# A new on-chip layout for the operands of a two-block transformer kernel

## The chip, the cores and the metric

The kernel runs on one core of a Trainium2 chip. TensorE (PE in the profile) multiplies, and its weight loads have a row of their own (PEld); VectorE (DVE), ScalarE (ACT) and GpSimd (POOL) do the element work; SyncE (SP) issues the transfers from the chip's memory. The metric is the device time of one execution in microseconds, lower being better.

## What is computed

The reference sends a sequence of 256 tokens with 1024 features through two transformer blocks, in float32. Cut to what matters:

```python
# first block
h = rmsnorm(x, norm_pre_mix);  z = h @ w_in           # gating, forgetting heads, memory heads
y = concat([gmlp(z), forgetting_attention(z), memory_cross_attention(z, mem)]) @ w_out
x = x + rmsnorm(y, norm_post_mix)
f = square(relu(rmsnorm(x, norm_pre_ffn) @ w_ff1)) @ w_ff2        # 1024 -> 4096 -> 1024
x = x + rmsnorm(f, norm_post_ffn)
# second block, two layers (sliding window attention, then latent attention)
for i in range(2):
    x = x + 0.5 * swiglu(rmsnorm(x), wg1[i], wu1[i], wd1[i])      # 1024 -> 2816 -> 1024
    x = x + attention_i(rmsnorm(x))
    x = x + 0.5 * swiglu(rmsnorm(x), wg2[i], wu2[i], wd2[i])
```

## The kernel before, in words

Activations are held transposed: 128 features in the partitions, the 256 tokens along them, so x is eight tiles of 128x256 float32 (1024 bytes a partition). Every large product is made of three matmuls, since each operand is split into a high and a low half of type float32r: high times high, high weight times low activation, low weight times high activation. These are lines 137 to 139 in `mm_t` (weight block of 128x128 stationary, 256 tokens moving) and lines 147 to 149 in `mm_n` (activation block stationary, 256 to 512 weight columns moving). Of 9048 matmuls in `mm_t`, 5520 with 128 columns of weights have the normed residual `xh`/`xl` moving, 2880 the hidden layer of a feed-forward stage `ah`/`al`, and 576 the joined heads `oh`/`ol`.

The weights are streamed. `Stream` takes transfers of up to 2048 columns into three buffers (`raw`), cuts them into parts of up to 1024 columns, and splits each part: ScalarE makes the high half `wh` (line 100), VectorE the low half `wl` (line 110). There are six buffers of each, and parts are asked for four ahead. A part is 24 matmuls in the gate and up stages. The order of the work on each engine is the order in which the code is written.

On-chip memory is a stack of pools. A pool starts where the one before it ends, each tile's size is rounded up to 32 bytes a partition, and the first pool starts at byte 16512 of a partition. The pools of a stage are opened behind the standing ones, and behind them all come at byte 138240, which is 270 times 512. In the kernel before, the pool of constants (`cst`) comes first, and in it `cols` has 404 bytes and `rows` 408. What stands behind them starts as follows (byte in a partition modulo 512, as the built programs have it):

| tiles | role in the products | before | after |
|---|---|---|---|
| `raw`, `wh`, `wl` | weights | 352 | 0 |
| `x`, `xh`, `xl` | residual and its halves | 352 | 0 |
| tiles of `tp` (`t`, `f`, `sq`, `acc`, `rb`) | work tiles | 352 | 0 |
| `ah`, `al`, `oh`, `ol`, `mh`, `ml`, `ch`, `cl` | activations of a stage | 0 | 0 |
| `kon` (identity, ones) | fp32 matmuls | 32 | 0 |
| `p`, `pt` of both attention layers of the second block (in the first block they are at 0 in both) | fp32 matmuls | 160 | 256 |
| `kT`, `qT` of the latent heads | fp32 matmuls | 160 | 256 |

So before, a matmul with `xh` or `xl` moving has both of its operands at 352, and one with `ah`, `al`, `oh` or `ol` moving has the moving operand at 0 and the weights at 352. In `mm_n` the weights move, at 352, and what is loaded is `xh` at 352 or `mh` and `ch` at 0.

Of the kernel before, what the change touches and what calls it, by code (L numbers as in the profile page):

```python
# [9 lines left out]
F32 = mybir.dt.float32  # L10
F32R = mybir.dt.float32r
BF16 = mybir.dt.bfloat16
I32 = mybir.dt.int32
# [4 lines left out]
P = 128  # L18
T = 256
# [4 lines left out]
CHUNK_COLS = 2048  # L24
# [11 lines left out]
N_COLS = 101  # L36
# [14 lines left out]
def block_kernel(ctx: ExitStack, tc: tile.TileContext, a: dict, out: bass.AP, upto: int = 99):  # L51
    nc = tc.nc
    pool = lambda name, bufs, **kw: ctx.enter_context(tc.tile_pool(name=name, bufs=bufs, **kw))
    cst = pool("cst", 1)
    wp = pool("wp", 1)
    res = pool("res", 1)
    tp = pool("tp", 2)
    sm = pool("sm", 1)
    psp = pool("psp", 8, space=bass.MemoryType.PSUM)
# [3 lines left out]
    def bank():  # L63
        return psp.tile([P, 512], F32, tag="ps", name="ps")

    # weight stream -------------------------------------------------------
    order = []
    RAW, HL, AHEAD = 3, 6, 4

    class Stream:  # L70
        """Weights come in transfers of up to CHUNK_COLS columns, each cut into parts; a part is
        split into float32r halves whose sum is the float32 weight."""

# [50 lines left out]
        def fill(self):  # L124
            """As many parts as there is room for, the low part of the last still to come."""
            while self.ns < self.ng + HL and self.split(gp):
                pass

    ws = Stream()

    # products ------------------------------------------------------------
    def mm_t(ps, w, off, n, x, kts, first, last, m=P):
        h, lo = w
        for j, k in enumerate(kts):
            c = off + k * n
            s0, s1 = first and j == 0, last and j == len(kts) - 1
            pe.matmul(ps, lhsT=h[:, c:c + m], rhs=x[0][k], start=s0, stop=False)  # L137
            pe.matmul(ps, lhsT=h[:, c:c + m], rhs=x[1][k], start=False, stop=False)  # L138
            pe.matmul(ps, lhsT=lo[:, c:c + m], rhs=x[0][k], start=False, stop=s1)  # L139
# [10 lines left out]

    # constants -----------------------------------------------------------
    ctx.enter_context(tc.manual_schedule())
# [3 lines left out]
    X = (xh, xl)  # L156
    cols = cst.tile([P, N_COLS], F32, name="cols")
    kon = cst.tile([P, 3 * P], F32, name="kon")
    kmask = cst.tile([P, 768], F32, name="kmask")
    rows = cst.tile([P, N_ROWS], F32, name="rows")  # L160
    posr = cst.tile([P, T], I32, name="posr")
    posc = cst.tile([P, 64], I32, name="posc")
    posn = cst.tile([P, 2], I32, name="posn")
    relb = cst.tile([P, 2, 16], F32, name="relb")
    mhalf = cst.tile([P, 32], F32, name="mhalf")
    gp.memset(mhalf, -0.5)
# [5 lines left out]
    def gcol(i, k):  # L172
        return cols[:, i * KT + k:i * KT + k + 1]
# [3 lines left out]

    # norms ---------------------------------------------------------------
    def rstd_pow(dst, src, n):
        gp.tensor_tensor(out=dst, in0=src, in1=mhalf[:, :n], op=ALU.pow)  # L180
# [4 lines left out]
    def add_sq(acc, k, src):  # L185
        if k == 0:
            act.activation(out=acc, in_=src, func=AF.Square)
        else:
            sq = tp.tile([P, T], F32, tag="sq", name="sq")
            act.activation(out=sq, in_=src, func=AF.Square)  # L190
            gp.tensor_tensor(out=acc, in0=acc, in1=sq, op=ALU.add)  # L191
# [50 lines left out]
    def prep(k, g, acc):  # L242
        """High part of a tile of the next normed input now, low part of the tile before."""
        act.activation(out=xh[k], in_=x[k], func=AF.Copy, scale=gcol(g, k))  # L244
        if acc is not None:
            add_sq(acc, k, x[k])
        prep_end()
        late.append((k, gcol(g, k)))

    def prep_end():  # L250
        while late:
            k, g = late.pop()
            dve.scalar_tensor_tensor(out=xl[k], in0=x[k], scalar=g, in1=xh[k].bitcast(F32), op0=ALU.mult, op1=ALU.subtract)

    # attention -----------------------------------------------------------
    def attn_exp(u):
# [68 lines left out]
    class Pipe:  # L325
        """Heads in flight: each step transposes the probabilities of the head two back, scores a
        new one, multiplies the values of the head three back, and goes on with the softmaxes."""

# [44 lines left out]

    # FFN of the second block ----------------------------------------------
    def ffn2(acc, gnext, extra=(), start=None, more=()):
# [52 lines left out]
    def out_proj_start(pipe, oh, ol, sets):  # L428
        """The first four tiles of an output projection, between the last steps of the heads."""
        ps, w, todo = [bank() for _ in range(4)], [], []  # L430
        seen = 0
        for ks in sets:
            for d in range(4):
                if not seen:
                    w.append(ws.get(max(0, HL - 2 - d)))
                mm_t(ps[d][:, :T], w[d], 0, P, (oh, ol), ks, not seen, False)
                pipe.done() or pipe.step()
            seen = 1
        while not pipe.done():
            pipe.step()  # L440
        return ps, w
# [28 lines left out]
    def y_evac(d, p, y, yacc, gi):  # L470
        """One tile of a post-normed sublayer: times its gain, and its squares."""
        if d == KT - 1:
            sq = tp.tile([P, T], F32, tag="sq", name="sq")
            act.activation(out=sq, in_=p, func=AF.Square)
        else:
            sq = None
            add_sq(yacc, d, p)
        act.activation(out=y[d], in_=p, func=AF.Copy, scale=gcol(gi, d))
        return sq

    # relative position bias: a threshold mask of the distances times the steps between buckets,
    # 8 groups of 4 keys a set, sets 0-3 for the first query tile
    rbd = cst.tile([P, 3, 64], BF16, name="rbd")

# [51 lines left out]

    # ======================================================================
    seq = [("w1f", 0, 4), ("w1q", 0, 6), ("w1k", 0, 2), ("w1m", 0, 1), ("w1v", 0, 2), ("w1u", 0, 3),
# [6 lines left out]
    for nm, i0, i1 in seq:  # L545
        for i in range(i0, i1):
            src = [a[nm][i, 0], a[nm][i, 1]] if len(a[nm].shape) == 4 else [a[nm][i]]
            for ap in src:
                n = ap.shape[-1]
                cut = cuts.get(nm) or ([DN_CUT * P, n] if nm.startswith("dn") else list(range(PART, n + 1, PART)))  # L550
                order.append((ap, cut))

# [1 line left out]
    warm_table(AF.Exp)  # L554
# [20 lines left out]
    with ExitStack() as es:  # L575
        mp = es.enter_context(tc.tile_pool(name="mix", bufs=1))
# [22 lines left out]

        # values and gates of the forgetting heads (natural)  # L600
        acc = new_acc()
# [16 lines left out]

        # queries and keys of the forgetting heads
        pq = [bank() for _ in range(3)]  # L620
# [98 lines left out]

        # queries of the memory heads, memory keys and values, with the forgetting heads in between  # L720
        for i in range(2):
# [22 lines left out]
        for tt in range(2):  # L744
            act.activation(out=vm[tt], in_=pv[tt][:, :T], func=AF.Copy, scale=rs_m[:, tt:tt + 1])
        # gating branch, with the memory heads in between
        pg = [bank(), bank()]
# [51 lines left out]

        # output projection, post norm  # L800
        yacc = new_acc("macc")
# [18 lines left out]

# [1 line left out]
    with ExitStack() as es:  # L822
# [69 lines left out]

# [1 line left out]
    with ExitStack() as es:  # L894
# [34 lines left out]
        mp = es.enter_context(tc.tile_pool(name="swa", bufs=1))  # L929
# [7 lines left out]
        rq = mp.tile([P, KT, 2, 2], F32, name="rq")  # L937
        ga = mp.tile([P, 1], F32, name="ga")
        dve.scalar_tensor_tensor(out=ga, in0=cols[:, C_AQ:C_AQ + 1], scalar=0.125, in1=cols[:, C_AK:C_AK + 1],
# [91 lines left out]

# [1 line left out]
    tq = cst.tile([P, 2, 2, 32], F32, name="tq")  # L1033
    tk = cst.tile([P, 2, 2, 32], F32, name="tk")

# [32 lines left out]
    with ExitStack() as es:  # L1068
        mp = es.enter_context(tc.tile_pool(name="mla", bufs=1))
# [10 lines left out]
        ol = [mp.tile([P, T], F32R, name=f"ol{k}") for k in range(KT)]  # L1080
        gb = mp.tile([P, 1], F32, name="gb")
        rqb = mp.tile([P, 4, 2, 4], F32, name="rqb")
# [3 lines left out]
        warm_table(AF.Exp)  # L1086
        # latent projections, transposed: keys and values first
        w, w2 = ws.get(), ws.get()
# [230 lines left out]

# [1 line left out]
def _kp(w):  # L1321
# [136 lines left out]
```

## Time and profile before

| what | value |
|---|---|
| time, median of 3 runs (lowest, highest) | 1299.66 us (1294.41, 1300.59) |
| span of the profiled execution, first to last instruction | 1296.4 us |
| TensorE's mean granted clock in it | 0.989 |
| PE busy | 1270.1 us (98%) |
| PEld busy | 1223.0 us (94%) |
| DVE busy | 846.0 us (65%) |
| ACT busy | 661.6 us (51%) |
| POOL busy | 197.4 us (15%) |
| DMA queue of the weights | 47.8% of 16 engines' span, 209.78 MB |

The profiled execution's own time is known as its span; the median of the runs lies 3.3 us above it, which is start and end outside the first and last instruction and the spread between runs. A busy PE does not tell how fast it is: matmuls are pipelined, one takes some 280 ns from its start to its modelled end and the next starts long before that. What tells is the step from one start to the next, read from the timeline, or the number of matmuls in a window.

### The profile page before, as it was taken

To read this page: it belongs to the slowest core of one execution; us is meant where nothing else is said; L and a number is where in the kernel's file an instruction comes from. 1 tells how busy PE (TensorE), PEld (TensorE's weight loads), DVE (VectorE), ACT (ScalarE), POOL (GpSimd) and SP (SyncE) were. 2 spreads that over 40 slices of the span, in tenths; PEclk is the share of its full clock that TensorE was granted. 3 is DMA by queue.
4 is the path that set the end of the run, shared out by engine and by line. 5 is a ranking of instruction groups with operands and counts; after the bars stand their busy time and mean duration, and the time that the engine had idled before them with its cause. 6 is when DMAs were issued, how large, how long until landed. Compare 5 with 4: busy or idle time off the path is not lost.

```text
span 1296.4 us, 24835 instructions
## 1 busy us (share of the span) xinstructions
PE 1270.1 (98%) x10316; PEld 1223.0 (94%) x10316; DVE 846.0 (65%) x1490; ACT 661.6 (51%) x1174; POOL 197.4 (15%) x192
## 2 busy tenths in 40 slices
PE   8999899999899999999999999999999999999998
PEld 7789899999799999977999999999999878999998
DVE  6886676654686666686766556666566786666553
ACT  5556455434344544565544444545444787444442
POOL 4424210110420001210300001100001451100000
PEclk9999899999899999999999999999999989999999
DMA  7534355565145545621555556545456412555453
GB/s 230 197 117 145 115 174 193 195 222 177 57 138 200 184 149 190 218 94 34 177 201 176 174 163 210 192 172 196 165 164 199 160 65 70 188 171 191 154 196 106
DMA packets 37265, 211.37 MB, mean 163 GB/s; under 512 B 4768, under 2 KB 8224, under 8 KB 18848
## 3 DMA queue, kind: packets, MB, share of 16 engines
q1 hardware_dynamic: 37152, 209.78, 47.8%
q8 instruction: 81, 1.33, 0.4%
q14 instruction: 32, 0.26, 0.1%
HBM read 208.71 MB, written 1.05 MB: 162 GB/s over the span
## 4 chain that ended last, share of the span: by engine, by line
PE 88%; DVE 7%; issue 2%; DMA 1%; ACT 1%; POOL 0%; SPq 0%; ACTq 0%; DVEq 0%; POOLq 0%
PE ps L137 26%; PE ps L138 26%; PE ps L139 26%; DVE wl L110 3%; PE ps L289 2%; PE ps L315 2%; PE ps L300 1%; PE ps L147 1%; PE ps L148 1%; PE ps L149 1%; DMA raw<-in_w1k 1%; PE ps L317 1%; DMA raw<-in_w1f 0%; DVE dg L226 0%; ACT wh L100 0%
## 5 line engine op out<-in xcount | busy, mean ns | idle before, releaser
L137 PE MATMUL ps<-xh,wh 128*128 128x256 f32 (+1 forms) x1848 | 529.6, 287 | 1.6 <-ACT xh L525 1.6
L138 PE MATMUL ps<-xl,wh 128*128 128x256 f32 (+1 forms) x1848 | 527.1, 285 | 1.4 <-DVE xl L532 0.9
L139 PE MATMUL ps<-xh,wl 128*128 128x256 f32 (+1 forms) x1848 | 525.7, 284 | 2.0 <-DVE wl L110 2.0
L110 DVE TENSOR_TENSOR wl<-raw,wh 128x1024 fp32r<-128x1024 f32 (+3 forms) x434 | 489.3, 1166 | 48.1 <-ACT wh L100 46.5
L100 ACT CAST wh<-raw 128x1024 fp32r<-128x1024 f32 (+4 forms) x436 | 400.2, 957 | 67.0 <-PE ps L138 28.6
L137 PEld LDWEIGHTS ps<-xh,wh 128*128 128x128 f32 (+1 forms) x1848 | 356.6, 193 | 5.3 <-issue 3.2
L138 PEld LDWEIGHTS ps<-xl,wh 128*128 128x128 f32 (+1 forms) x1848 | 356.5, 193 | 3.4 <-DVE xl L532 2.3
L139 PEld LDWEIGHTS ps<-xh,wl 128*128 128x128 f32 (+1 forms) x1848 | 356.8, 193 | 2.2 <-DVE wl L110 2.2
L137 PE MATMUL ps<-ah,wh 128*128 128x256 f32 x960 | 268.6, 280 | 0.0
L138 PE MATMUL ps<-al,wh 128*128 128x256 f32 x960 | 268.6, 280 | 0.0
L139 PE MATMUL ps<-ah,wl 128*128 128x256 f32 x960 | 268.5, 280 | 0.0
L137 PEld LDWEIGHTS ps<-ah,wh 128*128 128x128 f32 x960 | 180.5, 188 | 0.0
L138 PEld LDWEIGHTS ps<-al,wh 128*128 128x128 f32 x960 | 180.5, 188 | 0.0
L139 PEld LDWEIGHTS ps<-ah,wl 128*128 128x128 f32 x960 | 180.5, 188 | 0.0
L385 ACT ACTIVATE s<-t 128x256 f32<-128x256 f32 x88 | 36.8, 418 | 204.3 <-DVE t L383 204.3
L191 POOL TENSOR_TENSOR acc<-acc,sq 128x256 f32<-128x256 f32 x42 | 49.9, 1188 | 598.2 <-ACT sq L190 598.1
L383 DVE TENSOR_TENSOR t<-ps,rb 128x256 f32<-128x256 f32 x88 | 37.2, 423 | 85.4 <-PE ps L139 79.9
L205 DVE TENSOR_TENSOR al<-f,ah 128x256 fp32r<-128x256 f32 (+1 forms) x105 | 48.9, 466 | 52.8 <-ACT ah L204 52.8
L204 ACT CAST ah<-f 128x256 fp32r<-128x256 f32 (+1 forms) x105 | 45.9, 437 | 55.7 <-DVE f L387 43.1
L244 ACT ACTIVATE xh<-x,cols 128x256 fp32r<-128x256 f32 x40 | 20.4, 510 | 101.8 <-DVE x L420 94.7
L387 DVE TENSOR_TENSOR f<-ps,s 128x256 f32<-128x256 f32 x88 | 37.3, 424 | 47.4 <-ACT s L385 47.4
L419 DVE SCALAR_TENSOR_TENSOR t<-ps,rb 128x256 f32<-128x256 f32 x32 | 13.6, 424 | 77.1 <-PE ps L139 77.1
(285 smaller groups left out, 1322.8 us busy)
## 6 DMA issues: line engine op xcount, KB each, us to landing
raw<-in_gu SPq DMA_DIRECT2D x88, 1024.0 KB, 5.0
raw<-in_dn SPq DMA_DIRECT2D x64, 704.0 KB, 4.3
raw<-in_ff SPq DMA_DIRECT2D x32, 1024.0 KB, 4.9
raw<-in_w_out SPq DMA_DIRECT2D x4, 1024.0 KB, 4.9
raw<-in_aq SPq DMA_DIRECT2D x4, 1024.0 KB, 5.0
raw<-in_a_out SPq DMA_DIRECT2D x4, 1024.0 KB, 4.8
raw<-in_b_out SPq DMA_DIRECT2D x4, 1024.0 KB, 4.9
raw<-in_w1q SPq DMA_DIRECT2D x6, 512.0 KB, 3.9
```

What stands on the lines that cost most here:

```text
L100: act.copy(h[:, :n], t)
L110: eng.tensor_tensor(out=lo, in0=t, in1=h.bitcast(F32), op=ALU.subtract)
L137: pe.matmul(ps, lhsT=h[:, c:c + m], rhs=x[0][k], start=s0, stop=False)
L138: pe.matmul(ps, lhsT=h[:, c:c + m], rhs=x[1][k], start=False, stop=False)
L139: pe.matmul(ps, lhsT=lo[:, c:c + m], rhs=x[0][k], start=False, stop=s1)
L191: gp.tensor_tensor(out=acc, in0=acc, in1=sq, op=ALU.add)
L204: act.copy(h, src)
L205: dve.tensor_tensor(out=lo, in0=src, in1=h.bitcast(F32), op=ALU.subtract)
L289: pe.matmul(ps[:, o:o + n], lhsT=u["q"][:, i * P:i * P + P], rhs=u["k"][:, :n], start=True, stop=True)
L383: dve.tensor_tensor(out=t, in0=g, in1=rb, op=ALU.mult)
L385: act.activation(out=s, in_=t, func=AF.Silu)
L387: dve.tensor_tensor(out=f, in0=u, in1=s, op=ALU.mult)
```

## The change

No instruction is added, removed or moved on any engine, and every wait is for the same engine as before; only addresses differ. The small tiles whose sizes add up to 896 bytes come first in a pool of their own (`lead`), then the weight stream, the residual and the work tiles; the other constants follow those, the two of odd size (`cols`, `rows`) and `posn` last. `tq` and `tk` are allocated with them and not later. `ga` and `gb` are the first column of a tile of 32 columns. Comments and docstrings that go are left out here.

```diff
-    cst = pool("cst", 1)
+    lead = pool("lead", 1)
     wp = pool("wp", 1)
     res = pool("res", 1)
     tp = pool("tp", 2)
+    cst = pool("cst", 1)
     sm = pool("sm", 1)
...
-    cols = cst.tile([P, N_COLS], F32, name="cols")
+
+    mhalf = lead.tile([P, 32], F32, name="mhalf")
+    rbd = lead.tile([P, 3, 64], BF16, name="rbd")
+    relb = lead.tile([P, 2, 16], F32, name="relb")
+    posc = lead.tile([P, 64], I32, name="posc")
     kon = cst.tile([P, 3 * P], F32, name="kon")
     kmask = cst.tile([P, 768], F32, name="kmask")
+    posr = cst.tile([P, T], I32, name="posr")
+    tq = cst.tile([P, 2, 2, 32], F32, name="tq")
+    tk = cst.tile([P, 2, 2, 32], F32, name="tk")
+    cols = cst.tile([P, N_COLS], F32, name="cols")
     rows = cst.tile([P, N_ROWS], F32, name="rows")
-    posr = cst.tile([P, T], I32, name="posr")
-    posc = cst.tile([P, 64], I32, name="posc")
     posn = cst.tile([P, 2], I32, name="posn")
-    relb = cst.tile([P, 2, 16], F32, name="relb")
-    mhalf = cst.tile([P, 32], F32, name="mhalf")
...
-    rbd = cst.tile([P, 3, 64], BF16, name="rbd")
...
-        ga = mp.tile([P, 1], F32, name="ga")
+        ga = mp.tile([P, 32], F32, name="ga")[:, 0:1]
...
-    tq = cst.tile([P, 2, 2, 32], F32, name="tq")
-    tk = cst.tile([P, 2, 2, 32], F32, name="tk")
...
-        gb = mp.tile([P, 1], F32, name="gb")
+        gb = mp.tile([P, 32], F32, name="gb")[:, 0:1]
```

## Rows read from the trace of the kernel before

**Rows 1.** The page: span, busy time by engine, granted clock by slice

```profile
span 1296.4 us, 24835 instructions
...
PE 1270.1 (98%) x10316; PEld 1223.0 (94%) x10316; DVE 846.0 (65%) x1490; ACT 661.6 (51%) x1174; POOL 197.4 (15%) x192
...
PEclk9999899999899999999999999999999989999999
```

**Rows 2.** The chain of waits, shares of the span by line

```profile
by line: PE ps L137 26.0%; PE ps L138 25.7%; PE ps L139 25.5%; DVE wl L110 2.7%; PE ps L289 2.1%; issue 2.0%; PE ps L315 1.8%; PE ps L300 1.3%; PE ps L147 0.9%; PE ps L148 0.8%; PE ps L149 0.8%; DMA raw<-in_w1k 0.6%; PE ps L317 0.6%; DMA ra
```

**Rows 3.** Groups of PE instructions by shape: busy us, mean ns, idle before

```profile
L137 PE MATMUL ps<-xh,wh 128*128 128x256 f32 x1840 | 527.3, 287 | 1.6 <-ACT xh L525 1.6
...
L137 PE MATMUL ps<-ah,wh 128*128 128x256 f32 x960 | 268.6, 280 | 0.0
...
L137 PE MATMUL ps<-oh,wh 128*128 128x256 f32 x192 | 55.4, 288 | 0.0
```

**Rows 4.** Windows: length, then busy us and count (x) by engine, clock, DMA

```profile
160.00:220.00 60.00, 60.00 (x502) 60.00 (x502) 41.51 (x46) 34.52 (x50) 6.81 (x8) 1.00 0.55 186
255.00:315.00 60.00, 60.00 (x514) 60.00 (x513) 27.66 (x25) 24.67 (x33) 8.15 (x10) 1.00 0.55 195
655.00:735.00 80.00, 80.00 (x669) 80.00 (x669) 48.96 (x71) 37.92 (x56) 0.00 (x0) 1.00 0.54 185
955.00:1005.00 50.00, 50.00 (x429) 50.00 (x428) 32.59 (x45) 23.39 (x38) 7.44 (x6) 1.00 0.60 194
```

**Rows 5.** Timeline of PE, 1005 to 1010 us: starts; 32 columns of weights

```profile
1008.55 0.28 PE L139 MATMUL ps<-xh,wl 128*32 128x256 f32 x1
...
1009.91 0.28 PE L139 MATMUL ps<-xh,wl 128*32 128x256 f32 x1
```

**Rows 6.** Timeline of PE, 66 to 67.5 us: weights move, mh is loaded

```profile
65.79 0.29 PE L149 MATMUL ps<-wl,mh 128*128 128x256 f32 x1
...
67.47 0.28 PE L148 MATMUL ps<-wh,ml 128*128 128x256 f32 x1
```

**Rows 7.** Timeline of PE, 77 to 77.9 us: 384 columns move, xh is loaded

```profile
76.82 0.33 PE L148 MATMUL ps<-wh,xl 128*128 128x384 f32 x1
...
77.86 0.33 PE L148 MATMUL ps<-wh,xl 128*128 128x384 f32 x1
```

**Rows 8.** Timeline of PE, 1022.5 to 1024.8 us: 384 columns, ch loaded

```profile
1022.59 0.34 PE L147 MATMUL ps<-wh,ch 128*128 128x384 f32 x1
...
1024.53 0.34 PE L149 MATMUL ps<-wl,ch 128*128 128x384 f32 x1
```

**Rows 9.** The same at half clock: timeline, and its window

```profile
1042.65 0.52 PE L148 MATMUL ps<-wh,cl 128*128 128x384 f32 x1
...
1044.89 0.52 PE L149 MATMUL ps<-wl,ch 128*128 128x384 f32 x1
...
1042.20:1045.20 3.00, 3.00 (x11) 0.50 0.00 0
```

**Rows 10.** Groups of DVE and PE by shape: other operands by address

```profile
L205 DVE TENSOR_TENSOR al<-f,ah 128x256 fp32r<-128x256 f32 x90 | 38.2, 425 | 42.5 <-ACT ah L204 42.5
...
L387 DVE TENSOR_TENSOR f<-ps,s 128x256 f32<-128x256 f32 x88 | 37.3, 424 | 47.4 <-ACT s L385 47.4
...
L420 DVE TENSOR_TENSOR x<-x,t 128x256 f32<-128x256 f32 x32 | 13.6, 426 | 1.1
...
L315 PE MATMUL ps<-pt,av 128*64 128x256 f32 x32 | 10.3, 405 | 0.0
...
L315 PE MATMUL ps<-pt,fv 128*64 128x256 f32 x12 | 3.9, 405 | 0.0
```

**Rows 11.** The chain in order of time, 340 to 400 us, its longest pieces

```profile
363.26 3.97 DVE wl L110 x2
370.69 3.97 DVE wl L110 x2
378.13 3.97 DVE wl L110 x2
```

## The prediction

> **What bounds the kernel now.** I read the page first: PE is busy 98% of a span of 1296.4 us, at full clock in nearly every slice [rows 1]. That alone says little, so the chain of waits comes next: lines 137 to 139, the three matmuls of the split products, hold 26.0 + 25.7 + 25.5 = 77.2% of the span, 1001 us, and no line of another engine, nor any transfer, holds more than 2.7% [rows 2]. The kernel is as fast as those matmuls follow each other. Their listed durations (280 to 288 ns) are not that pace, but the groups already differ by what moves, and `xh` stands at 352 where `ah` and `oh` stand at 0 [rows 3]. The pace comes from counts. A window counts whatever touches it, so its length plus one duration (0.28 us), divided by the count, is the step from start to start [rows 4]:
> - `xh`/`xl` moving at 352, weights at 352: 60.28 / 502 and 80.28 / 669, both 120.0 ns;
> - `ah`/`al` moving at 0, weights at 352: 60.28 / 514 and 50.28 / 429, both 117.3 ns.
>
> Clock, shape, type, weights and bytes are the same in the two; what differs is where the moving tile starts. So the layout does reach the pace, and 2.7 ns of it is visible before any change.
>
> **What an aligned step would be.** At half clock 384 columns step by 2.24 us over 7 steps, 320.0 ns, one column per cycle with nothing on top [rows 9]. At full clock one column per cycle would be 106.7 ns for 256 columns and 160 ns for 384, and no step of these products comes down to it: something that half the pace hides costs 10 to 16 ns. The sizes tell more. With weights of only 32 columns and both operands at 352 the step is 1.36 us over 12, 113.3 ns [rows 5]; with 128 columns 120.0 ns [rows 4]; 384 columns moving with both at 352 take 1.04 us over 6, 173.3 ns [rows 7]. Above one column per cycle these are 6.7, 13.3 and 13.3 ns: one or two times 16 columns, that is 64 bytes. 352 is 5.5 times 64. My reading is that the moving operand is fetched in pieces of 64 bytes: 1024 bytes that start in the middle of a piece touch 17, not 16, and 128 columns of weights cost one piece-time more. 16 + 1 + 1 = 18 pieces give 120.0, 17 without the second give 113.3, and 1536 bytes (25 pieces, plus 1) give 173.3. That fits all three rows where both operands stand at the same offset.
>
> Where the two stand at different offsets the step isn't a whole number of pieces: 117.3 ns is 17.6, and 384 columns moving at 352 over `ch` at 0 take 1.94 us over 11, 176.4 ns, which is more than 173.3 although one of the operands is better aligned [rows 8]. With 256 columns of weights moving at 352 over `mh` at 0 it is 1.68 us over 14, again 120.0 [rows 6]. So aligning the loaded operand alone gains nothing; the moving one alone gains 2.7 ns; both together, which is what the change makes, stand in no row. Bounds for both at 0: below, 106.7 ns (one column per cycle); above, 120.0 (what a common offset gives now). I take 113.3, which is 16 pieces plus the one for the weights: a common offset gave whole pieces in all three rows, and the half piece at the front goes.
>
> **The change part by part.**
> - `mm_t` over `xh`/`xl`, 5520 matmuls: 120.0 to 113.3, 6.7 ns each.
> - `mm_t` over `ah`, `al`, `oh`, `ol`, 3456 matmuls: 117.3 to 113.3, 4.0 ns each.
> - How many of them set the end: at the mean step of (5520 x 120.0 + 3456 x 117.3) / 8976 = 119.0 ns the chain's 1001 us are 8410 matmuls, 94% of all. So 0.94 x (5520 x 6.7 + 3456 x 4.0) = 0.94 x (37.0 + 13.8) = 48 us.
> - `mm_n` is under 3% of the chain (0.9 + 0.8 + 0.8) [rows 2], much of it waits at the start. At 4 to 6% of 2.5% of the span it gives 1 us or 2; I count 0, which leaves this on the safe side.
> - fp32 matmuls (scores, transposes, values): nothing. `pt` at 160 and `pt` at 0 both read 405 ns over 256 columns [rows 10]; they have the pace at which nothing shows.
> - VectorE and ScalarE: nothing. Operands at 352 and 0 mixed, PSUM and 0, or all at 352 read 425, 424 and 426 ns [rows 10].
> - Transfers into `raw`: no row separates their address, but the chain holds under 1% of such waits by line (0.6% for the largest) [rows 2], so even a tenth of those is near 1 us; I take 0.
> - Earlier `tq`, `tk` and wider `ga`, `gb`: no instruction and no wait differs, 0.
>
> What is late next: the split of the weights. While the buffers refill after the first block's feed-forward stage, pairs of `wl` instructions set the pace [rows 11]; such stretches are outside the 94%, yet a faster PE lengthens them. In steady stretches VectorE is busy 41.5 of 60 and 49.0 of 80 us [rows 4]; 6% less time lifts the higher from 69% to 73%, so it keeps up. I take 2 us off for the refills: 46 us. The sum is against the span of 1296.4, which becomes 1250.4; the median of the runs lies 3.3 us above that span, so the forecast is 1254 us. Its own range, for 112.5 to 114.5 ns and a path share of 85 to 97%, is 1243 to 1268.
>
> **The rivals.**
> 1. Only the moving operand counts: all products go as `ah` does now. For it: a rate of 117.3 on 2880 matmuls without exception, and `mh`, where aligning the loaded tile changed nothing. Against it: the broken 17.6 pieces, which only unequal offsets show. 0.94 x 5520 x 2.7 = 14 us, 1286.
> 2. No piece is lost at all, 106.7 to 111 ns. For it: the 32-column rows lose none to their weights. Against: they are a quarter of the load. At 109 ns: 0.94 x (5520 x 11.0 + 3456 x 8.3) = 84 us, 1216; at the bound of 106.7 1196. The Trainium skill ("TensorE: Matmul & The Clock Gate", Part 2) states two independent read ports, so that loading the next weights takes nothing from the running matmul, and a step of N/2.4 + 2.5 ns, 109.2 here; by it the sum would be this rival's. The rows disagree: narrower weights alone took 6.7 ns off.
> 3. Slower: two operands at a common offset collide, wherever that is. For it: `xh` over `wh`, both at 352, is the slowest pace and the steadiest. Then the `xh` products stay at 120.0, and those over `ah` and `oh`, which lose their unequal offset, go from 117.3 to 120.0: 0.94 x 3456 x 2.7 = 9 us more, 1309. Against it: `mh` at 0 under weights at 352 has unequal offsets and is at 120.0 too. It decides if the step in the hidden-layer stages rises above 117.3.
> 4. Nothing happens: 1300. An offset of 352 would have to be as good as 0. The comparison of `xh` and `ah` speaks against it, unless their 2.7 ns come from something else that differs between the stages, such as eight tiles used over and over. The Trainium skill ("SBUF — State Buffer", Specifications) gives lines of 16 bytes; 352 is 22 of them, so by this rule no operand moves onto a better boundary. The windows show otherwise as far as they go, 120.0 against 117.3.
>
> **How the numbers follow.** Forecast (113.3 ns) 0.45; a step between it and rival 1, around 115.5 ns and 1271 us, 0.07; rival 1 0.20; rival 2 0.13; rival 3 0.10; rival 4 0.05. A measurement of this kernel can tell about 0.5%, 6.5 us, from no change. Faster: 0.45 + 0.07 + 0.20 + 0.13 = 0.85; same is rival 4, 0.05; slower is rival 3, 0.10. The range runs from 1208, which takes in most of rival 2, to 1290, which takes in rival 1; outside stay rivals 3 and 4 and the rest of 2, under 0.2.
>
> **What would show it.** In the profile after, a window in a gate and up stage and one in a hidden-layer stage should have the same step, 113.3 ns, and it should be as even as the 120.0 is now: 532 matmuls in 60 us where there were 502 and 514. The chain should still be lines 137 to 139. The attention stages and the start should hardly move. I am wrong in the step if the two windows differ or if both read 117.3 or 120.0; wrong in the path if the step is 113.3 and the time falls by much less than 46 us, in which case the idle time before the `xh` products, now 1.6 us at line 137 [rows 3], has grown under `wl` or `raw`.

## The result, and the profile after

The changed kernel takes 1304.77 us (median of 5 runs, 1303.69 to 1305.42), the kernel before in the same series 1297.97 us (5 runs, 1294.41 to 1300.59). The ratio is 1.0057 with a 95% interval of 1.0039 to 1.0074: slower by 0.6%, where 1254 us had been forecast. That is the way of the third rival, which was priced at 1309 us and given a chance of 0.10.

The page of the changed kernel, span and busy time by engine:

```profile
span 1301.9 us, 24835 instructions
...
PE 1276.5 (98%) x10316; PEld 1230.6 (95%) x10316; DVE 846.3 (65%) x1490; ACT 661.7 (51%) x1174; POOL 196.1 (15%) x192
```

Against [rows 1] the span is 5.5 us longer, PE is busy 6.4 us longer and its weight loads 7.6 us; VectorE, ScalarE and GpSimd agree to about 1 us. The chain of waits by line (the product's lines are now 138 to 140):

```profile
by line: PE ps L138 26.3%; PE ps L139 26.0%; PE ps L140 25.9%; PE ps L294 2.2%; DVE wl L111 2.1%; issue 2.0%; PE ps L320 1.8%; PE ps L305 1.3%; PE ps L148 0.9%; PE ps L149 0.8%; PE ps L150 0.8%; DMA raw<-in_w1q 0.7%; PE ps L322 0.6%; DMA x<
```

Still the products, 78.2% where [rows 2] had 77.2%. Two groups of them by shape, and the four windows of [rows 4] (length, then busy us and count by engine, clock, DMA):

```profile
L138 PE MATMUL ps<-xh,wh 128*128 128x256 f32 x1840 | 526.6, 286 | 1.0 <-ACT xh L528 1.0
...
L138 PE MATMUL ps<-ah,wh 128*128 128x256 f32 x960 | 271.7, 283 | 0.0
```

```profile
160.00:220.00 60.00, 60.00 (x503) 60.00 (x502) 41.81 (x46) 34.53 (x50) 6.79 (x8) 1.00 0.54 188
255.00:315.00 60.00, 60.00 (x503) 60.00 (x502) 27.67 (x25) 23.65 (x30) 7.69 (x9) 1.00 0.53 187
655.00:735.00 80.00, 80.00 (x669) 80.00 (x668) 49.25 (x70) 37.46 (x56) 0.00 (x0) 1.00 0.55 188
955.00:1005.00 50.00, 50.00 (x419) 50.00 (x418) 31.55 (x46) 23.04 (x39) 6.35 (x6) 1.00 0.56 187
```

With `xh` moving nothing has changed: 669 in 80 us, 120.0 ns. With `ah` moving, 419 in 50 us where there were 429: 50.28 / 419 = 120.0 ns in place of 117.3, and a duration of 283 ns in place of 280 [rows 3]. Both kinds of product are now equally slow, which is the sign of a wrong step that the prediction named. The third rival's price for that, 0.94 x 3456 x 2.7 ns, is 9 us; 5.5 us show in the spans and 6.8 us between the medians.

### The profile page after: what moved, and what is told of

Read it like the earlier page. It is cut to its first block, busy times and chain, and to the rows that moved or that the text cites. A ratio compares the mean times of both kernels' runs of the same rounds, so it can differ in the third digit from the quotient of the medians.

```text
span 1301.9 us, 24835 instructions
## 1 busy us (share of the span) xinstructions
PE 1276.5 (98%) x10316; PEld 1230.6 (95%) x10316; DVE 846.3 (65%) x1490; ACT 661.7 (51%) x1174; POOL 196.1 (15%) x192
## 4 chain that ended last, share of the span: by engine, by line
PE 89%; DVE 6%; issue 2%; ACT 1%; DMA 1%; POOL 0%; SPq 0%; ACTq 0%; POOLq 0%; DVEq 0%
PE ps L138 26%; PE ps L139 26%; PE ps L140 26%; PE ps L294 2%; DVE wl L111 2%; PE ps L320 2%; PE ps L305 1%; PE ps L148 1%; PE ps L149 1%; PE ps L150 1%; DMA raw<-in_w1q 1%; PE ps L322 1%; DMA x<-in_x 0%; DVE dg L231 0%; ACT wh L101 0%
## 5 line engine op out<-in xcount | busy, mean ns | idle before, releaser
L139 PE MATMUL ps<-al,wh 128*128 128x256 f32 x960 | 271.7, 283 | 0.0
L138 PE MATMUL ps<-ah,wh 128*128 128x256 f32 x960 | 271.7, 283 | 0.0
L140 PE MATMUL ps<-ah,wl 128*128 128x256 f32 x960 | 271.7, 283 | 0.0
L138 PEld LDWEIGHTS ps<-ah,wh 128*128 128x128 f32 x960 | 184.3, 192 | 0.0
L140 PEld LDWEIGHTS ps<-ah,wl 128*128 128x128 f32 x960 | 184.3, 192 | 0.0
L139 PEld LDWEIGHTS ps<-al,wh 128*128 128x128 f32 x960 | 184.3, 192 | 0.0
```

## Experiments

The theory after this result: the step depends on the offset between the moving operand and the weights, not on where either of them starts. Its rivals: the number of pieces that an operand touches (the reading of the prediction), and something in the stages themselves. The excerpts of code below have comments added and leave out the tiles that give the gaps their sizes.

### Trains of matmuls at chosen offsets

```diff
+        for a, d, m, n in scans:
+            ps = bank()
+            for i in range(48):
+                b, c = 128 * (i % 8), ...          # next weights block, next moving tile
+                pe.matmul(ps[:m, :n], lhsT=scan_w[:, a + b:a + b + m], rhs=scan_v[:, d + c:d + c + n],
+                          start=i == 0, stop=i == 47)
```

> The changed kernel with trains of 48 float32r matmuls added behind the last product (they write junk to free PSUM banks, read nothing back; the output is computed as before). Each train has its own byte offset modulo 512 for the loaded operand (a) and the moving one (b), its own width of weights and number of moving columns; the step from start to start is read from the trace. Theory 1, a common offset locks the step: a = b gives 120.0 ns at 0, 16 and 32 bytes alike; b different from a gives a broken step with a mean near 117.3 ns. If pieces of 64 bytes are what counts, b - a of 64, 128, ... reads 120.0 again and all of 32, 96, 160, ... read 117.3; if larger banks count, the step differs among multiples of 64 too. Theory 2, the number of pieces touched: a = 0 with b = 0 is never slower than any other (it is at 120.0, so nothing is under 120.0 here, and 117.3 needs weights at 352). Theory 3, the stage and not the address made the 117.3 (the many tiles of a hidden layer): every train reads the same. Narrower weights (32, 64, 96 columns) at a common offset: 113.3, then in steps up to 120.0. Two bytes an element (bf16): at or under 109 ns, with no dependence on b, if the bytes are what is short.

PE's windows inside eight of the trains (length, busy us and count, clock, DMA). In order: weights and moving tiles at 0; moving at 192; at 256; then at 0 again with 32 and with 64 columns of weights; 96 columns with the moving tiles at 32; 512 columns moving at 0; bf16 in place of float32r.

```profile
1303.50:1308.50 5.00, 5.00 (x44) 1.00 0.07 26
1337.50:1342.50 5.00, 5.00 (x46) 1.00 0.00 0
1348.70:1353.70 5.00, 5.00 (x44) 1.00 0.00 0
1445.50:1450.50 5.00, 5.00 (x47) 1.00 0.00 0
1456.80:1461.30 4.50, 4.50 (x42) 1.00 0.00 0
1473.50:1478.40 4.90, 4.90 (x44) 1.00 0.00 0
1495.90:1505.90 10.00, 10.00 (x46) 1.00 0.01 2
1517.80:1522.40 4.60, 4.60 (x45) 1.00 0.00 0
```

A window of 5 us is only good to one matmul, so the steps come from the starts in the trace, as the mean from the seventh matmul of a train on. In the table the weights stand at 0:

| moving minus weights, bytes modulo 512 | 0 | 32 | 64 | 96 | 128 | 160 | 192 | 224 |
|---|---|---|---|---|---|---|---|---|
| step, ns | 120.0 | 116.7 | 117.8 | 120.0 | 118.7 | 117.4 | 113.3 | 118.3 |
| the same at 256 bytes more | 120.0 | 117.8 | 117.8 | 120.0 | 118.6 | 118.6 | 117.8 | 118.3 |

Both at 32 bytes read 119.9, both at 16 bytes 118.4. The moving tiles at 4 bytes read 123.3, at 8 bytes 120.0. At offset 0, weights of 32, 64, 96 and 128 columns step 113.3, 113.3, 116.0 and 120.0 ns; 384 and 512 moving columns under 128 of weights step 173.3 and 226.7 ns; bf16 steps 109.2 ns in both of its trains, whose offsets are 32 bytes apart. At an offset of 32 bytes, weights of 32, 64 and 96 columns step 117.4, 119.0 and 116.6 ns, and 384 and 512 moving columns 173.3 and 233.3 ns.

What follows: the stage isn't the cause, since trains of one code in one place differ by 7 ns. Counting pieces is wrong too: 128 columns of weights read 120.0 with both operands at 0, as `xh` over `wh` did with both at 352, so there was no half piece at the front to win. At a common offset the cost over one column per cycle is 6.7 ns with 32 or 64 columns of weights and 13.3 ns with 128, and it is 13.3 for 256, 384 and 512 moving columns alike: there it goes with the weights that are loaded meanwhile. At 32 bytes that order is gone: 64 columns of weights (119.0) are slower than 128 (116.7). In bf16, with half the bytes, all but 2.5 ns of the cost vanishes. Two things that were expected did not come: unequal offsets do not share one pace near 117.3, and both operands at 16 bytes are not at 120.0.

The table also explains the rows of before. `xh` over `wh` has offset 0 (120.0), `ah` at 0 over weights at 352 has 160 (117.3 in the kernel, 117.4 here), and weights at 352 moving over `mh` at 0 have 352, that is 256 and 96 (120.0 here and in [rows 6]).

### Residual aligned, weights left at 352

```diff
     wp = pool("wp", 1)
+    gap = pool("gap", 1)          # 160 bytes: xh, xl to 0 modulo 512
     res = pool("res", 1)
...
     sm = pool("sm", 1)
+    gap2 = pool("gap2", 1)        # 352 bytes: the pools of the stages stay at 0
```

> The kernel before with one thing moved: the residual and work tiles (xh, xl, x, t, f, ...) start at 0 modulo 512, the weights stay at 352, so all moving operands stand at 0 over weights at 352 as the hidden layers did before. Theory 1 (unequal offsets are the faster): the products over xh step 117.3 ns as those over ah do, 0.94 x 5520 x 2.7 ns = 14 us less than before, 1284 us. Theory 2 (weights at 352 with a moving operand at 0 is good for its own sake): the same here, told apart by the scan. Theory 3 (the stage, not the address): xh stays at 120.0 and the time at 1298 us.

1293.4 us (12 runs) against 1296.03 (17 runs), ratio 0.998 with an interval of 0.9965 to 0.9995. Its windows, from a run of 1296.92 us:

```profile
160.00:220.00 60.00, 60.00 (x514) 60.00 (x513) 43.35 (x47) 35.16 (x50) 6.83 (x8) 1.00 0.53 178
255.00:315.00 60.00, 60.00 (x514) 60.00 (x513) 27.66 (x25) 23.69 (x30) 7.69 (x9) 1.00 0.54 194
655.00:735.00 80.00, 80.00 (x677) 80.00 (x676) 49.64 (x70) 38.20 (x56) 0.00 (x0) 1.00 0.54 185
955.00:1005.00 50.00, 50.00 (x419) 50.00 (x418) 31.68 (x44) 22.69 (x37) 7.46 (x6) 1.00 0.58 191
830.00:910.00 80.00, 80.00 (x669) 80.00 (x669) 53.83 (x98) 39.00 (x59) 0.00 (x0) 1.00 0.53 184
```

In the first stage `xh` does step 117.3 ns (514 in 60 us), as expected. But with the very same offset of 160 it steps 118.6 at 655 us and 120.0 at 830 us, and `ah`, whose addresses relative to the weights are those of the kernel before, steps 120.0 at 955 us where it stepped 117.3. The last two belong together: from 828 to 1008 us both `xh` and `ah` hold 120.0. So an offset has more than one pace, and of 14 us expected 3 came. The runs also scatter more (1290.0 to 1300.2).

### The kernel's own product, three starts for each offset

```diff
+        for rep in range(3):
+            for d in range(0, 128, 8):
+                ...                                # 1, 3 or 5 short bf16 matmuls ahead
+                xs = ([sc_x[:, d + T * k:d + T * k + T] for k in range(KT)], [sc_y[...] for k in range(KT)])
+                for r in range(2):
+                    mm_t(ps[:, :T], (sc_h, sc_l), 0, P, xs, range(KT), True, True)
```

> The changed kernel with trains of 48 matmuls behind the last product, this time through the kernel's own mm_t (high over high, high over low, low over high, eight blocks of 512 bytes of weights and eight moving tiles of 1024 bytes, twice), output as before, the trains' results unused. The moving tiles stand at d = 0, 32, ..., 480 bytes modulo 512 over weights at 0; every offset is run three times, behind one, three or five short bf16 matmuls, so that the train starts in another phase. Theory 1a, the offset sets the step: the three trains of an offset agree, 120.0 at 0 and 256, 113.3 at 192, 116.7 to 119 elsewhere, as in the first scan. Theory 1b, the offset and the phase in which a train starts set it together: the three trains of some offsets differ by 3 ns or more (which would explain why the layout of the run half stepped 117.3 in one stage and 118.5 to 120.0 in others). Under 1b the order of the addresses matters too, and 192 need not be at 113.3.

Starts of PE at offset 192, the first and the second of its three trains (the second and the last matmul of each):

```profile
1343.09 0.29 PE L139 MATMUL ps<-sc_y,sc_h 128*128 128x256 f32 x1
...
1348.32 0.28 PE L140 MATMUL ps<-sc_x,sc_l 128*128 128x256 f32 x1
...
1439.74 0.28 PE L139 MATMUL ps<-sc_y,sc_h 128*128 128x256 f32 x1
...
1445.15 0.28 PE L140 MATMUL ps<-sc_x,sc_l 128*128 128x256 f32 x1
```

46 steps each: 5.23 us, 113.7 ns with the run-in (113.3 after it), and 5.41 us, 117.6 ns (117.8 after it). Same code, same offset, another start: 4.5 ns apart. So theory 1b holds: the offset and the start set the pace together. Offset 0 gives 120.0 from every start, 64 gives 117.8, 96 gives 120.0; 128 and 160 have two paces each (118.6 and 120.0; 117.3 and 118.7), and so have 32 (116.7 and 117.8) and 192. Offsets that differ by 256 gave the same paces.

### All moving operands at 192

```diff
     wp = pool("wp", 1)
+    gap = pool("gap", 1)          # 192 bytes
     res = pool("res", 1)
```

> The changed kernel with 192 bytes left free between the weights and the residual: all moving operands of mm_t (xh, xl, ah, al, oh, ol) at 192 modulo 512 over weights at 0. Theory 1a: 113.3 ns in every stage, 0.94 x (5520 x 6.7 + 3456 x 4.0) = 48 us under the kernel before, 1249 us. Theory 1b: the single good train at 192 was one phase of its own; the stages step 115 to 119 and differ from each other, 1275 to 1292 us. If only equal against unequal offsets counts: 117.3, 1284 us.

1257.88 us (4 runs, 1255.08 to 1260.42) against 1296.66 (7 runs): ratio 0.9711, interval 0.9691 to 0.9732. This beats both kernels, and it lies between what was expected of one pace everywhere (1249) and of mixed paces (from 1275). Its page and its windows:

```profile
span 1253.2 us, 24835 instructions
...
PE 1225.1 (98%) x10316; PEld 1179.1 (94%) x10316; DVE 845.7 (67%) x1490; ACT 660.6 (53%) x1174; POOL 196.1 (16%) x192
```

```profile
160.00:220.00 60.00, 60.00 (x527) 60.00 (x526) 43.68 (x48) 35.80 (x51) 5.88 (x7) 1.00 0.57 193
255.00:315.00 60.00, 60.00 (x511) 60.00 (x511) 30.30 (x28) 24.76 (x31) 5.69 (x7) 1.00 0.58 208
655.00:735.00 80.00, 80.00 (x708) 80.00 (x707) 50.64 (x75) 38.51 (x59) 0.00 (x0) 1.00 0.54 181
480.00:530.00 50.00, 50.00 (x442) 50.00 (x441) 33.75 (x51) 25.83 (x44) 9.48 (x8) 1.00 0.64 222
```

The third window steps 80.28 / 708 = 113.4 ns, the second 60.28 / 511 = 118.0. By the starts, the products hold the slow pace from 206 to 318 us without a break, `xh` up to 228 us and then `ah`, and from 625 to 978 us they keep the fast one but for some 4 us. Those 4 us on PE:

```profile
800.40 0.50 PE L218 MATMUL ps<-kon,acc 128*128 128x1 f32 x4
...
801.08 0.28 PE L141 MATMUL ps<-xh,wl 128*128 128x256 f32 x1
...
803.44 0.28 PE L140 MATMUL ps<-xl,wh 128*128 128x256 f32 x1
803.67 0.60 PE L238 MATMUL ps<-dg,kon 128*128 128x256 f32 x2
...
804.70 0.28 PE L141 MATMUL ps<-xh,wl 128*128 128x256 f32 x1
...
805.72 0.28 PE L141 MATMUL ps<-xh,wl 128*128 128x256 f32 x1
```

It is 20 steps of 118.0 ns behind one kind of fp32 matmul, then 9 of 113.3 ns behind another. That is no accident of this place: in this trace and in that of `x192` below, all 14 stretches of `xh` behind `kon` over `acc` step 117.8 ns, and 9 of 10 behind `dg` over `kon` step 113.3. So a stretch keeps its pace until other matmuls come in between, the change from `xh` to `ah` does not end it, and what runs just ahead decides much of which pace it is. The neighbouring values of the sum fit: mean steps of 114.1 ns for `xh`, 114.5 for `ah` and 117.3 for `oh` make 0.94 x (5520 x 5.9 + 2880 x 2.8 + 576 x 0.6) = 39 us against before, and 38.8 were measured.

### Finer offsets, and two controls

For the first control the gap of 192 bytes goes ahead of the weights; for the second it is 256 bytes behind them:

```diff
+    gap = pool("gap", 1)          # all192: 192 bytes
     wp = pool("wp", 1)
...
     wp = pool("wp", 1)
+    gap = pool("gap", 1)          # d256: 256 bytes
     res = pool("res", 1)
```

> As scan2, but finer around the good offset: the moving tiles at 160, 168, 176, 184, 188, 192, 196, 200, 208, 216, 224, 240 and 448 bytes modulo 512 over weights at 0, each four times, behind one, two, three or four short bf16 matmuls. If the step follows the offset modulo 256 and the starting phase together, 448 and 192 behave alike, each at 113.3 in some trains and 117.8 in others, and offsets within 16 bytes of 192 may hold the 113.3 more often. If 192 is one narrow spot, its neighbours read 117 to 120 always.

> The changed kernel with the same 192 bytes left free, but ahead of the weights and not behind them, so that weights and moving operands all stand at 192 modulo 512. If the offset between the two is what counts: 120.0 ns in every stage as in the changed kernel, 1304 us. If it is the moving operand's own place that counts: as d192, 113 to 118 ns and 1258 us.

> The changed kernel with 256 bytes left free between weights and residual, all moving operands at 256 modulo 512 over weights at 0. If the offset modulo 256 is what counts: 120.0 ns in every stage, 1304 us, as without the gap. If the offset modulo 512 counts, or if any gap helps, it is below 1290 us.

With everything at 192 the kernel takes 1303.97 us (ratio 1.0079, 1.0054 to 1.0103), with the moving operands at 256 1305.63 us (1.0082, 1.0065 to 1.01). One window of each, the first with everything at 192, the second with the moving operands at 256:

```profile
655.00:735.00 80.00, 80.00 (x669) 80.00 (x668) 49.41 (x70) 37.46 (x56) 0.00 (x0) 1.00 0.54 189
```

```profile
655.00:735.00 80.00, 80.00 (x669) 80.00 (x668) 49.22 (x69) 38.11 (x56) 0.00 (x0) 1.00 0.54 186
```

Both step 120.0, as the changed kernel does. So it is the offset between the two operands, modulo 256, and neither the place of one of them nor the gap as such. This is shown with weights at 0, 32, 192 and 352, all multiples of 32 as every tile here is; with weights at 16 bytes the first scan read 118.4 at offset 0 in its one train, so there the place may count too.

The finer trains: 168, 176, 184, 188, 196, 200 and 216 bytes all read 118.6 to 122.2 ns, 208 read 116.7 once and 119.2 otherwise, 240 read 117.1. Of the eight trains at 192 and 448, five were at 113.3 and three at 117.8; over all three scans it is 8 at 113.3 of 17. The good offset is a single spot, and about half of the trains miss it.

### One kind of product at a time

The gap of 192 bytes before the residual alone (`x192`, with 320 bytes behind `sm` that bring the stages' pools back to 0), and behind `sm` alone (`h192`).

> The changed kernel with the residual and its halves (xh, xl) and the work tiles at 192 modulo 512, and the hidden layers and heads (ah, al, oh, ol) left at 0 over weights at 0. If the offset acts product by product: xh steps about 114.2 ns (113.3 with stretches at 117.8, as in the run d192) and ah stays at 120.0, so the saving against the changed kernel is 0.94 x 5520 x 5.8 ns = 30 us, 1274 us. If the sum of steps is not what the time follows, or if one stage's state carries over to the next, it is elsewhere.

> The reverse: the stage pools (ah, al, oh, ol and the attention tiles) at 192 modulo 512, xh and xl at 0 with the weights. Expected by the same working: ah at about 114.6, xh at 120.0, 0.94 x 3456 x 5.4 ns = 18 us less than the changed kernel, 1287 us; the two savings together should be the 47 us that both offsets gave in the run d192.

1273.59 us (ratio 0.9828, 0.9804 to 0.9851) and 1287.34 us (0.9923, 0.99 to 0.9947), for 1274 and 1287 expected. A window in a gate and up stage and one in a hidden-layer stage, first with `xh` moved, then with `ah` moved:

```profile
640.00:740.00 100.00, 100.00 (x885) 100.00 (x884) 65.56 (x94) 50.35 (x75) 0.00 (x0) 1.00 0.55 190
750.00:800.00 50.00, 50.00 (x419) 50.00 (x418) 32.46 (x45) 24.27 (x40) 7.75 (x6) 1.00 0.58 190
```

```profile
640.00:740.00 100.00, 100.00 (x836) 100.00 (x835) 63.22 (x89) 48.55 (x71) 0.00 (x0) 1.00 0.53 182
750.00:800.00 50.00, 50.00 (x443) 50.00 (x442) 32.70 (x47) 24.22 (x42) 6.34 (x5) 1.00 0.58 189
```

113.3 and 120.0 ns in the one, 120.0 and 113.5 in the other. Each kind of product follows its own offset. Each run reckoned from the kernel before in its own series, the savings against the changed kernel are 29.0 and 15.3 us; together 44.3, where moving both saves 45.6.

## Why the prediction was wrong, point by point

- **What bounds the kernel** was right. The chain stayed on the three lines, PE's pace moved with the layout, and the busy time of VectorE, ScalarE and GpSimd moved by no more than about 1 us.
- **The step that failed is the aligned step**: "a common offset gave whole pieces in all three rows, and the half piece at the front goes". The three rows were read as counts of 64-byte pieces of the moving operand, one of them lost to a start in mid-piece. With both operands at 0, where 113.3 ns was forecast, `xh` and `ah` measured 120.0 ns, as `xh` did with both at 352. The even pace at a common offset wasn't a sign of anything lost at the front; it is the pace of the common offset, wherever that lies. The 113.3 ns that later came at an offset of 192 are no support for the count of pieces: moving tiles at 64, 128 and 256 start on a whole piece as well and step 117.8 to 120.0.
- **One of the three rows is no common offset.** The blocks of 32 columns in [rows 5] lie 128 bytes apart in their tile (`c = off + k * n` with n = 32), so only every second one stands at the moving tile's place modulo 256.
- **The comparison under it was confounded.** `xh` and `ah` differ in where the moving tile starts, and by that also in its offset to the weights. I took the first for the cause. The product over `mh` should have warned: the tile that starts at 0 gained nothing there. Its offset is 352, that is 256 and 96, and 96 steps 120.0 in every train.
- **The rival that came true** had its mechanism and its price: `ah` and `oh` at 120.0, 9 us, of which 5.5 to 6.8 showed. "Against it" stood that `mh` has unequal offsets and is at 120.0 too; that is no argument, since unequal offsets have paces from 113.3 to 123 ns. That `oh` had the 117.3 of `ah` was assumed from its place: no window held it, and by the starts of the trace before its mean step was 117.9.
- **The price per nanosecond** was right. 0.94 of the products set the end: with it the runs with one kind of product moved came within 1 us of what was expected of them, and the 113.3 ns that were predicted, once they were reached in most stages, took 39 us off. The low end of the forecast's own range, 1243, leaves out the 2 us of the refills; with them it is 1245.
- **What was costed at nothing** showed nothing: `pt` still reads 405 ns over 256 columns, VectorE and ScalarE are busy as long as before, and the largest wait for a transfer has 0.7% of the chain where it had 0.6%. The refills could not be tested by a slower PE; in the faster kernel with all moving operands at 192, `wl` has 2.5% of the chain where it had 2.7% [rows 2], so they did not grow.
- **The rules of the Trainium skill** weighed then: "TensorE: Matmul & The Clock Gate", Part 2, says that the next weights' load takes nothing from the running matmul, and its gap of N/2.4 + 2.5 ns, which it gives for a matmul by itself, is 109.2 ns for 256 columns. bf16 agrees, 109.2 in two trains. float32r does not: 113.3 to 123 ns, by the offset and, at a common offset, by the width of the weights.

What stays open: how what runs ahead of a start leads to 113.3 or 117.8 at an offset of 192, and why the run with weights at 352 held 120.0 for 180 us, which no train at its offset showed. Why the offset counts at all is not shown. That the load of the next weights collides with the reads of the running matmul is a conjecture: it rests on the widths at a common offset and on bf16, the widths at 32 bytes do not follow it, and it was not tried by itself.

## What to carry to other kernels

Read a product's pace from counts in a window, not from durations. Where two groups differ in an address, list the addresses of both operands before naming a cause, and test the place of each apart from the offset between them. When full-rate float32r products bound a kernel, leave a gap between the weights and the moving tiles and try its size: 192 bytes gave 3% here, and offsets of 0 and 256 cost 0.6 to 0.8%. A few odd offsets (4, 196, 216 bytes) were slower than a common one, and with 512 moving columns 32 bytes were slower than 0, so the 192 is a find for 256 columns and not a rule.

## What the runs showed of the hardware

- The step of 128x128 by 256 float32r products, clock granted in full, lies between 113.3 and 123.3 ns, by the offset of the moving operand from the weights modulo 256 bytes (weights at multiples of 32): 120.0 at 0, 113.3 or 117.8 at 192, 123.3 at 4 bytes.
- At some offsets there are two paces, at 160 three (117.3 and 118.7 in the trains, 120.0 in a kernel); a stretch of matmuls keeps the one in which it started, for over 100 us, until other matmuls come in between. At 192 it was 117.8 ns in 14 of 14 stretches behind the fp32 sums (`kon` over `acc`), 113.3 in 9 of 10 behind `dg` over `kon`.
- bf16 operands of the same shape step 109.2 ns at both offsets tried.
